# A quarter's shift and scale as one 512-wide row product, and four other edits, in a one-core transformer block

## The chip, the cores and the metric

The kernel runs on one core of one Trainium2 chip. The metric is device time in microseconds (us) of the whole program: the median of 3 runs before is 2113.18 us (2111.8 to 2114.73). Five engines work side by side: TensorE (PE, with its weight loads shown as PEld), VectorE (DVE), ScalarE (ACT), GpSimd (POOL) and SyncE (SP, which here only issues DMAs). Each has its own list of instructions and waits on semaphores for the others. Matrix products are written to PSUM, in tiles of up to 128 partitions x 512 floats; everything else on the core lives in SBUF.

## The reference, cut to what matters

```python
cond = jax.nn.silu(c)
mod = (cond @ ada_w[l] + ada_b[l]).reshape(B, N_SUBLAYERS, 3, D_MODEL)
h = modulate(x, norm_g[l, 0], mod[:, 0, 0], mod[:, 0, 1])      # rms_norm(x) * g * (1 + scale) + shift
x = x + 0.5 * mod[:, 0, 2][:, None, :] * swiglu(h, ffn1_w1[l], ffn1_w3[l], ffn1_w2[l])
h = modulate(x, norm_g[l, 1], mod[:, 1, 0], mod[:, 1, 1])
y = hybrid_mixer(h, ...)     # FoX attention and DSA attention, two gates, output product
x = x + mod[:, 1, 2][:, None, :] * y
h = modulate(x, norm_g[l, 2], mod[:, 2, 0], mod[:, 2, 1])
x = x + 0.5 * mod[:, 2, 2][:, None, :] * swiglu(h, ffn2_w1[l], ffn2_w3[l], ffn2_w2[l])
```

The model width D is 1024, there are 1024 positions, and the feed-forward width is 2816. `mod` needs nine 1024-wide products of one row (`cond`) with `ada_w`, 4 MB for each of the nine. All of it is float32.

## The kernel before, in words

**Layout.** x is held transposed: eight tiles of 128 channels, each in two halves of 512 positions (`x[c][half]`). A precise product is made of three reduced-precision ones (`mm3`): each operand is split into a high part `wh` or `h` (ACT rounds it) and a low part `wl` or a second `h` (DVE subtracts). These products read a float32r type; a few small ones are taken in plain float32: the row products of the modulation, the column sums of the norm and the spreading of the norm factor. The two feed-forward layers use Strassen-like block products with seven operands (`Operands`, `UpPair`, `Down`).

**Who sets the order.** The kernel records all operations of a stage in a `Plan` and then places them engine by engine with its own cost table (`Plan.length`, durations in us) before it emits them. Each engine then runs that fixed list. All instructions show one line, L198, in the profile, so they are told apart by tile names. Within the first stage the DMA issues of SP are kept in the written order up to `nc.inorder = False`.

**The start.** SP first loads `c` (tile `cond`), then the eight first halves of x (256 KB each). ACT's queue loads `ada_b` and `ng`. ACT makes Silu of `cond` and squares the x tiles (`nacc`, `nsq`), DVE adds the squares, and PE sums them over partitions by four products with `ones_col`; DVE makes the inverse root (`nv`, `na`, `nr`, twelve small operations one after another), and PE spreads it over all partitions by four products with `ident`. The result is `rb`.

Before the first layer can start, shift and scale of the first 256 channels are needed (quarter 0: x tiles 0 and 1), and soon after, those of quarter 1 (tiles 2 and 3). For each quarter eight 256 KB loads bring 1024 rows x 256 columns of `ada_w` twice, for shift (i = 0) and scale (i = 1). In the kernel before, `ModQuarter.row` makes the shift on PE: eight float32 products of one weight column (`cond`) with 256 columns of `mraw`, accumulated in one row; ACT copies the row (`mrow`) and two products with `ones_col` turn it into columns. `ModQuarter.add` makes the scale on DVE: eight multiply-adds over 128 x 256 (`macc`), summed over partitions by two products. `mod_done` adds the bias and, for the scale, forms A = (1 + scale) * g.

Then `Operands.block(c)` makes the operand pair: DVE computes x = x * A * rb in one pass, ACT the high part h = x + shift, DVE the low part. From then on PE runs `y<-h,wh` and `y<-h,wl` products of the first layer.

**The end of attention.** `attention` walks blocks j of 256 positions for pairs of heads; `att_values` turns the weights (`pt`, then `pth` on ACT and `ptl` on DVE), multiplies them with the values (`vst`) into a PSUM tile `py` of two buffers, which the gates share, and takes it out by ACT and DVE (`yt`). The first operation of the next stage is the last gate, 24 products into a bank of tag `b`.

**The end.** `Down.run` finishes the last feed-forward layer. In its last pass (p = 6) the last 3 of 11 weight pairs are done block by block: 9 products of 512 columns, one `xc` operation on DVE, and a 256 KB store to the output.

Of the kernel before, what the change touches and what calls it, by code (L numbers as in the profile page):

```python
# [23 lines left out]
D = 1024  # L24
# [153 lines left out]
class Plan:  # L178
# [111 lines left out]
    def length(self, t, e):  # L290
# [1167 lines left out]
def attention(k, p, kind, npairs, out, ps2, ps_t, ps_y):  # L1458
# [79 lines left out]
class ModQuarter:  # L1538


    N = 256

    def __init__(self, k, i, q, bank):
        self.k, self.i, self.q, self.bank, self.raws = k, i, q, bank, []

    def load(self, g):
        k, n = self.k, self.N
        t = t512(k, name="mraw")
        c0 = self.i * D + self.q * n
        k.nc.sync.dma_start(t.rearrange("p (a n) -> p a n", a=2),  # L1550
                            k.ada_w[g * 256:g * 256 + 256, c0:c0 + n].rearrange("(a p) n -> p a n", p=128))
        self.raws += [t[:, 0:n], t[:, n:2 * n]]

    def add(self):
        k, nc = self.k, self.k.nc
        acc = t512(k, name="macc")[:, 0:self.N]
        for kc, t in enumerate(self.raws):
            c = k.cond[:, kc:kc + 1]
            if kc == 0:
                nc.vector.tensor_scalar(acc, t, c, None, op0=ALU.mult)  # L1560
            else:
                nc.vector.scalar_tensor_tensor(acc, t, c, acc, op0=ALU.mult, op1=ALU.add)
        self.done(acc, k.ones_col)

    def row(self):
        k, nc = self.k, self.k.nc
        t = self.bank()[0:1, 0:self.N]
        for kc, r in enumerate(self.raws):
            nc.tensor.matmul(t, k.cond[:, kc:kc + 1], r, start=kc == 0, stop=kc == 7)
        r = t512(k, name="mrow")[0:1, 0:self.N]  # L1570
        nc.scalar.activation(r, t, AF.Copy)
        self.done(r, k.ones_col[0:1, :])

    def done(self, v, one):
        t = self.bank()
        for b in range(2):
            self.k.nc.tensor.matmul(t[:, b:b + 1], v[:, b * 128:b * 128 + 128], one, start=True, stop=True)
        mod_done(self.k, self.i, t, 2 * self.q, 2)
# [32 lines left out]
class Operands:  # L1611
# [26 lines left out]
    def block(self, c):  # L1638

        self.scale(c, 0)  # L1640
        self.pair("b11" if c < 4 else "b21", self.x[c][0], self.shift(c), "h0")

# [237 lines left out]
class Down:  # L1880
# [87 lines left out]
    def run(self, steps={}):  # L1968

        k = self.k  # L1970
        for p, (first, _, early) in enumerate(self.ORDER):
# [11 lines left out]
            def mms(d, q):  # L1983
                w, m = ops[q]
                c = slice(d * 128, d * 128 + 128)
                mm3(k, ps[d], w[0][:, c], w[1][:, c], *m, new and q == 0, q == PAIRS - 1, skip_group_check=True)
# [17 lines left out]
            for d in range(4):  # L2004
                for q in range(together, PAIRS):
# [217 lines left out]
def layer(tc, xT, c, pos, ada_w, ada_b, ng, inv, w13a, w2a, w_a, w_f, w_q, w_g, fb, fg, dg, wbr, wout, w13b, w2b, out):  # L2223
    with ExitStack() as es:
# [64 lines left out]
        with ExitStack() as ph:  # L2289
# [24 lines left out]
            quarter = [[ModQuarter(k, i, q, bank) for i in range(2)] for q in range(2)]  # L2314
# [49 lines left out]
            for i in range(8):  # L2364
# [4 lines left out]
                                    channel_multiplier=1)  # L2369
            sq = SquareSum(k, nc.vector)  # L2370
# [5 lines left out]
            for n in range(4):  # L2376
                for m in quarter[0]:
                    m.load(n)
            for i in range(2):
                pairs[i].load1("c", (0,))  # L2380
            for n in range(4):
                for m in quarter[1]:
                    m.load(n)
# [3 lines left out]
            rms[0] = norm_rms(k, sq.acc, rp, bank)  # L2387
            ops.rb[0] = norm_spread(k, rms[0], bank)
# [160 lines left out]
        with ExitStack() as ph:  # L2549
# [10 lines left out]
            def dsa():  # L2560
# [4 lines left out]
                yield from attention(k, ap, "dsa", 4, k.d_y[1], p2, pt, py)  # L2565
# [11 lines left out]
        with ExitStack() as ph:  # L2577
# [19 lines left out]
            last_gate(k, w_g[15], bank)  # L2597
# [37 lines left out]
            for _ in rest:  # L2635
# [6 lines left out]
                        lambda t, i, j: lambda: nc.sync.dma_start(out[i, :, j * H:j * H + H], t), nc.vector)  # L2642
# [75 lines left out]
```

## Time and profile before

| What | Value |
|---|---|
| median of 3 runs | 2113.18 us (2111.8 to 2114.73) |
| profiled execution, its own time | 2112.17 us |
| its span, first to last instruction | 2110.5 us |
| PE busy | 2094.6 us, 10296 records |
| DVE, ACT, POOL busy | 1641.7, 1135.6, 251.1 us |
| first `y<-h,wh` product of the first layer | 20.89 us |
| last product ends, DVE's last operation starts | 2106.57 us |

The profiled execution is 1.67 us longer than its span (what lies around the program) and 1.01 us shorter than the median of the runs. A record is one row of the trace. One float32r product leaves one record. PE's busy time counts the modelled ends of pipelined products; the distance between starts tells the true pace.

### The profile page before, as it was taken

How to read it: one execution, taken by the hardware profiler on the slowest of the kernel's cores; microseconds unless marked ns; L12 is line 12 of the kernel's file. 1: busy time of each engine (PE TensorE's matmuls, PEld its weight loads, DVE VectorE, ACT ScalarE, POOL GpSimd, SP SyncE). 2: the span in 40 equal slices, each digit the busy share in tenths (PEclk: the TensorE clock that was granted, in tenths of full speed). 3: DMA queues.
4: the chain of work that ended last, by engine and by line, in shares of the span. 5: the costliest groups of instructions: out<-in, count | busy, mean ns of one | idle time of the engine just before them, and what ended most of it. 6: DMA issues, size and time to landing. Idle time of an engine off the chain costs nothing.

```text
span 2110.5 us, 30999 instructions
## 1 busy us (share of the span) xinstructions
PE 2094.6 (99%) x10296; PEld 1728.2 (82%) x10296; DVE 1641.7 (78%) x3167; ACT 1135.6 (54%) x2075; POOL 251.1 (12%) x397
## 2 busy tenths in 40 slices
PE   8999999999999999999999999999999999999999
PEld 5887888888888888888888888888888888888887
DVE  7989887869977399886998877979975765568554
ACT  5754444445456266688776776335543333334443
POOL 0022222321100000000444332000000000000000
PEclk9999999999999999999999999999999999999999
DMA  9468888899721555668543224794142523375511
GB/s 347 134 215 275 303 295 274 277 379 366 261 92 48 172 174 192 217 244 274 192 158 99 86 66 160 252 315 154 46 130 100 194 85 129 101 264 206 189 50 41
DMA packets 218285, 398.72 MB, mean 189 GB/s; under 512 B 27198, under 2 KB 69694, under 8 KB 217100
## 3 DMA queue, kind: packets, MB, share of 16 engines
q1 hardware_dynamic: 199772, 339.24, 48.0%
q0 software_dynamic: 18064, 57.46, 7.1%
q8 instruction: 81, 1.33, 0.3%
q14 instruction: 80, 0.66, 0.1%
q10 hardware_dynamic: 288, 0.05, 0.0%
HBM read 282.62 MB, written 114.03 MB: 188 GB/s over the span
## 4 chain that ended last, share of the span: by engine, by line
PE 91%; issue 3%; DVE 2%; DMA 2%; ACT 1%; POOL 1%; SPq 0%; POOLq 0%; DVEq 0%; ACTq 0%
PE b L198 37%; PE y L198 28%; PE pj L198 12%; PE py L198 7%; PE p L198 4%; PE pt L198 4%; DMA mraw<-in_ada_w 0%; POOL d_g L198 0%; DMA f<-d_f 0%; DMA wr<-in_w13b 0%; ACT nt L198 0%; DMA d_wf10l<-pre 0%; DVE z L198 0%; DMA x<-in_xT 0%; ACT h L198 0%
## 5 line engine op out<-in xcount | busy, mean ns | idle before, releaser
L198 PE MATMUL b<-h,wh 128*128 128x512 f32 x1408 | 436.5, 390 | 0.5 <-DVE z L198 0.4
L198 PE MATMUL y<-h,wh 128*128 128x512 f32 x1280 | 397.1, 390 | 0.4 <-ACT h L198 0.3
L198 ACT ACTIVATE wh<-wr 128x512 fp32r<-128x512 f32 x308 | 192.6, 629 | 316.0 <-PE b L198 166.1
L198 PEld LDWEIGHTS b<-h,wh 128*128 128x128 f32 x1408 | 263.2, 188 | 59.1 <-DVE z L198 3.4
L198 PEld LDWEIGHTS y<-h,wh 128*128 128x128 f32 x1280 | 239.6, 188 | 53.4 <-issue 1.2
L198 DVE TENSOR_TENSOR wl<-wr,wh 128x512 fp32r<-128x512 f32 x308 | 208.4, 686 | 94.4 <-ACT wh L198 88.8
L198 PE MATMUL b<-h,wl 128*128 128x512 f32 x704 | 273.6, 389 | 0.0
L198 PE MATMUL y<-h,wl 128*128 128x512 f32 x640 | 249.0, 389 | 0.0
L198 PE MATMUL pj<-wh,h 128*128 128x512 f32 x512 | 161.3, 391 | 0.0
L198 PEld LDWEIGHTS b<-h,wl 128*128 128x128 f32 x704 | 132.2, 188 | 27.7
L198 PEld LDWEIGHTS y<-h,wl 128*128 128x128 f32 x640 | 120.1, 188 | 24.8
L198 ACT ACTIVATE wh<-g 128x512 fp32r<-128x512 f32 x154 | 96.0, 624 | 80.2 <-PE b L198 55.7
L198 PE MATMUL b<-wh 128*128 128x512 f32 x352 | 137.0, 389 | 0.7 <-ACT mrow L198 0.7
L198 DVE TENSOR_TENSOR wl<-a,wh 128x512 fp32r<-128x512 f32 x132 | 90.8, 688 | 59.9 <-ACT wh L198 55.7
L198 PE MATMUL b<-wl,wh 128*128 128x512 f32 x352 | 136.9, 389 | 0.0
L198 PE MATMUL b<-wh,wl 128*128 128x512 f32 x352 | 136.8, 389 | 0.0
L198 ACT ACTIVATE wh<-a 128x512 fp32r<-128x512 f32 x132 | 82.4, 625 | 99.9 <-PE b L198 60.3
L198 DVE TENSOR_TENSOR wl<-g,wh 128x512 fp32r<-128x512 f32 x154 | 105.6, 686 | 29.6 <-ACT wh L198 29.1
L198 POOL TENSOR_SCALAR pr<-pr,mn 128x128 f32<-128x128 f32 (+7 forms) x128 | 102.3, 816 | 167.3 <-DVE mn L198 135.1
L198 ACT ACTIVATE pth<-pt 128x512 fp32r<-128x512 f32 (+1 forms) x160 | 85.5, 554 | 55.9 <-PE pt L198 54.3
L198 DVE TENSOR_TENSOR ptl<-pt,pth 128x512 fp32r<-128x512 f32 (+1 forms) x160 | 97.9, 632 | 20.1 <-ACT pth L198 18.6
L198 PEld LDWEIGHTS pj<-wh,h 128*128 128x128 f32 x512 | 95.7, 188 | 18.6
(382 smaller groups left out, 4376.4 us busy)
## 6 DMA issues: line engine op xcount, KB each, us to landing
g<-d_g SPq DMA_DIRECT2D x154, 256.0 KB, 5.3
mraw<-in_ada_w SPq DMA_DIRECT2D x144, 256.0 KB, 5.7
wr<-in_w13a SPq DMA_DIRECT2D x112, 256.0 KB, 5.4
wr<-in_w13b SPq DMA_DIRECT2D x88, 256.0 KB, 4.8
d_g<-z POOLq DMA_DIRECT2D x77, 256.0 KB, 5.8
d_g<-z SPq DMA_DIRECT2D x77, 256.0 KB, 3.2
a<-in_w2a SPq DMA_DIRECT2D x44, 256.0 KB, 6.3
a<-in_w2b SPq DMA_DIRECT2D x44, 256.0 KB, 5.3
```

The costliest lines, as they stand in the source:

```text
L198: getattr(getattr(self.tc.nc, engine), op)(*map(real, a), **{n: real(v) for n, v in kw.items()})
```

## The change

Six edits, and one entry of the planner's cost table.

- `ModQuarter` is replaced by `Quarters`: a load now brings 128 rows with 256 columns of shift and 256 of scale side by side, and PE makes both in one row of 512 by eight float32 products. Nothing of it is left on DVE. ACT copies the 512-wide row, four products turn it into columns, and `mod_done` is called for scale and shift.
- x * rb (`normed`) is done before A is known. After A, ACT makes h = x * A + shift directly from it, and DVE makes x * A apart and then the low part (`rounded`). This holds for x tiles 0 to 3.
- `cond` is loaded by ACT's queue, `ada_b` and `ng` by POOL's; SP begins with x.
- The value products of the last block of DSA attention go to a half of a `p2` tile and not to `py`; the last gate uses a bank of tag `y`.
- The last block of the last pass is done in two halves of 256 columns, each with its own DVE operation and 128 KB store.
- The planner's cost of a plain float32 product becomes max(0.112, 0.005 + n / 1200) us for n columns; it was max(0.224, 0.009 + n / 595), with 1200 in place of 595 for a one-row result.

```diff
-                d = max(0.224, 0.009 + n / (595.0 if t.rows > 1 else 1200.0))
+                d = max(0.112, 0.005 + n / 1200.0)
...
-    yield from att_values(k, p, *pend, ps_t, ps_y)
+    yield from att_values(k, p, *pend, ps_t, ps_last or ps_y)
...
-class ModQuarter:
...
+class Quarters:
+    def load(self, kc):
+        k, c = self.k, self.q * 256
+        t = t512(k, name="mraw")
+        src = k.ada_w[kc * 128:kc * 128 + 128, 0:2 * D].rearrange("p (i n) -> p i n", i=2)
+        k.nc.sync.dma_start(t.rearrange("p (i n) -> p i n", i=2), src[:, :, c:c + 256])
+        self.raws.append(t)
+
+    def sums(self):
+        t = self.bank()
+        for kc, w in enumerate(self.raws):
+            nc.tensor.matmul(t[0:1, :], k.cond[:, kc:kc + 1], w, start=kc == 0, stop=kc == 7)
+        self.row = t512(k, name="mrow")[0:1, :]
+        nc.scalar.activation(self.row, t[0:1, :], AF.Copy)
+
+    def columns(self):
+        for b in range(4):
+            nc.tensor.matmul(t[:, b:b + 1], r[:, b * 128:b * 128 + 128], k.ones_col[0:1, :], start=True, stop=True)
+        for i in (1, 0):
+            mod_done(k, i, t[:, 2 * i:2 * i + 2], 2 * self.q, 2)
...
+    def normed(self, c):
+        t = self.x[c][0]
+        self.k.nc.vector.tensor_mul(t, t, self.rb[0])
+
+    def rounded(self, c):
+        nc.scalar.activation(a, t, AF.Identity, bias=shift, scale=scale)
+        self.x[c][0] = x = t512(k, name="x")
+        nc.vector.tensor_scalar(x, t, scale, None, op0=ALU.mult)
+        nc.vector.scalar_tensor_tensor(b, x, shift, a.bitcast(F32), op0=ALU.add, op1=ALU.subtract)
...
+                if p == 6 and self.s == 2 and d == 3:
+                    for i in range(2):
+                        cs = slice(i * 256, i * 256 + 256)
+                        for q in range(together, PAIRS):
+                            mms(d, q, (cs,))
+                        k.nc.vector.scalar_tensor_tensor(t[:, cs], ps[d][:, cs], g, t[:, cs], op0=ALU.mult, op1=ALU.add)
+                        self.done(t[:, cs], d, 1, i)()
+                    break
...
-        k.cond = const_in([128, 8], "cond", c)
-        k.ada_b = const_in([128, 72], "ada_b", ada_b, nc.scalar)
-        k.ng = const_in([128, 24], "ng", ng, nc.scalar)
+        k.cond = const_in([128, 8], "cond", c, nc.scalar)
...
+            k.ada_b = const_in([128, 72], "ada_b", ada_b, nc.gpsimd)
+            k.ng = const_in([128, 24], "ng", ng, nc.gpsimd)
...
-            for m in quarter:
-                m[1].add()
-                m[0].row()
+            for c in range(2):
+                ops.normed(c)
+            quarter[0].columns()
+            for c in range(2, 4):
+                ops.normed(c)
+            quarter[1].sums()
+            quarter[1].columns()
             for c in range(4):
-                ops.block(c)
+                ops.rounded(c)
...
-                yield from attention(k, ap, "dsa", 4, k.d_y[1], p2, pt, py)
+                yield from attention(k, ap, "dsa", 4, k.d_y[1], p2, pt, py, lambda: p2()[:, 0:H])
...
-            last_gate(k, w_g[15], bank)
+            last_gate(k, w_g[15], k.seed_bank)
```

Since the planner sets the order, the lists of the engines move too. The middle of the program (mixer projections, indexer, top-k and nearly all of attention) keeps its order. Two places matter below.

PE at the start, from the first row product on (`mraw` is the loaded piece of `ada_w`, `nacc` the sum of squares, `nr` the norm factor, `mrow` and `macc` the results that are turned into columns). Before:

```order
L198 MATMUL b<-mraw,cond 1x256 x2
L198 MATMUL b<-ones_col,nacc 128x1 x4
L198 MATMUL b<-mraw,cond 1x256 x6
L198 MATMUL b<-ones_col,mrow 128x1 x2
L198 MATMUL b<-ident,nr 128x128 x4
L198 MATMUL b<-ones_col,macc 128x1 x2
L198 MATMUL b<-mraw,cond 1x256 x2
L198 MATMUL y<-h,wh 128x512 x2
L198 MATMUL b<-mraw,cond 1x256 x2
L198 MATMUL y<-h,wh 128x512 x3
```

Now:

```order
L198 MATMUL b<-ones_col,nacc 128x1
L198 MATMUL b<-mraw,cond 1x512
L198 MATMUL b<-ones_col,nacc 128x1 x3
L198 MATMUL b<-mraw,cond 1x512 x5
L198 MATMUL b<-ident,nr 128x128 x2
L198 MATMUL b<-mraw,cond 1x512
L198 MATMUL b<-ident,nr 128x128 x2
L198 MATMUL b<-mraw,cond 1x512
L198 MATMUL b<-ones_col,mrow 128x1 x4
L198 MATMUL y<-h,wh 128x512
L198 MATMUL b<-mraw,cond 1x512
L198 MATMUL y<-h,wh 128x512
```

All eight products of quarter 0 now stand ahead of the first `y<-h,wh`, at twice the width, and the first of them behind a product that waits for the sum of squares. Before, quarter 0 had its eight at 256 columns there and quarter 1 its first two. The eight of quarter 1 now stand singly between the first `y` products.

PE at the end of attention (`pr` are the weights to be turned, `gw` is the last gate's weight). Before:

```order
L198 MATMUL pt<-ident,pr 128x128 x2
L198 MATMUL py<-ptl,vst 64x256
L198 MATMUL py<-ptl,vst 64x128
L198 MATMUL pt<-ident,pr 128x128 x3
L198 MATMUL py<-pth,vst 128x256 x2
L198 MATMUL py<-pth,vst 128x128
L198 MATMUL py<-ptl,vst 64x256
L198 MATMUL py<-ptl,vst 64x128
L198 MATMUL py<-pth,vst 128x128
L198 MATMUL py<-ptl,vst 64x256
L198 MATMUL py<-ptl,vst 64x128
L198 MATMUL b<-h,gw 128x512 x24
```

Now:

```order
L198 MATMUL pt<-ident,pr 128x128 x3
L198 MATMUL py<-ptl,vst 64x256
L198 MATMUL py<-ptl,vst 64x128
L198 MATMUL py<-pth,vst 128x128
L198 MATMUL p_14551<-pth,vst 128x256 x2
L198 MATMUL p_14551<-pth,vst 128x128
L198 MATMUL p_14551<-ptl,vst 64x256
L198 MATMUL p_14551<-ptl,vst 64x128
L198 MATMUL p_14551<-ptl,vst 64x256
L198 MATMUL p_14551<-ptl,vst 64x128
L198 MATMUL p_14551<-pth,vst 128x128
L198 MATMUL y<-h,gw 128x512 x24
```

The last eight value products go to another tile and end with a `pth` product, where before they ended with two `ptl` products. On ACT the two takings-out (`yt`) now stand behind all `pth` copies; before, one stood between them.

More of the change, by code (lines that the diff above doesn't have):

```diff
@@ L1455, in pair_heads, with attention @@
     k.ready = heads
-def attention(k, p, kind, npairs, out, ps2, ps_t, ps_y):
+def attention(k, p, kind, npairs, out, ps2, ps_t, ps_y, ps_last=None):
     pend = ()
@@ L1535, in steps @@
         mod_done(k, self.i, cols, 4 * self.h, 4)
-class ModQuarter:
[L1541 to L1547, printed above, removed]
-        t = t512(k, name="mraw")
[L1549 to L1554, printed above, removed]
-        k, nc = self.k, self.k.nc
[L1556 to L1574, printed above, removed]
-        t = self.bank()
-        for b in range(2):
-            self.k.nc.tensor.matmul(t[:, b:b + 1], v[:, b * 128:b * 128 + 128], one, start=True, stop=True)
-        mod_done(self.k, self.i, t, 2 * self.q, 2)
@@ new lines, with __init__ @@
+class Quarters:
+    def __init__(self, k, q, bank):
+        self.k, self.q, self.bank, self.raws = k, q, bank, []
+    def load(self, kc):
+        k, c = self.k, self.q * 256
+        t = t512(k, name="mraw")
+        src = k.ada_w[kc * 128:kc * 128 + 128, 0:2 * D].rearrange("p (i n) -> p i n", i=2)
+        k.nc.sync.dma_start(t.rearrange("p (i n) -> p i n", i=2), src[:, :, c:c + 256])
+        self.raws.append(t)
+    def sums(self):
+        k, nc = self.k, self.k.nc
+        t = self.bank()
+        for kc, w in enumerate(self.raws):
[3 more added lines that the diff above has]
+    def columns(self):
+        k, nc, r = self.k, self.k.nc, self.row
+        t = self.bank()
[3 more added lines that the diff above has]
+            mod_done(k, i, t[:, 2 * i:2 * i + 2], 2 * self.q, 2)
@@ L1641, in block @@
         self.pair("b11" if c < 4 else "b21", self.x[c][0], self.shift(c), "h0")
+    def normed(self, c):
+        t = self.x[c][0]
+        self.k.nc.vector.tensor_mul(t, t, self.rb[0])
+    def rounded(self, c):
+        k, nc, t, i = self.k, self.k.nc, self.x[c][0], self.s * 8 + c
+        scale, shift = k.A[:, i:i + 1], self.shift(c)
+        a, b = t512(k, F32R, "h", "h0"), t512(k, F32R, "h", "h0")
+        nc.scalar.activation(a, t, AF.Identity, bias=shift, scale=scale)
+        self.x[c][0] = x = t512(k, name="x")
+        nc.vector.tensor_scalar(x, t, scale, None, op0=ALU.mult)
+        nc.vector.scalar_tensor_tensor(b, x, shift, a.bitcast(F32), op0=ALU.add, op1=ALU.subtract)
+        k.B["b11"].append((a, b))
     def first(self):
@@ L1981, in run, with mms @@
             ops = []
-            def mms(d, q):
+            def mms(d, q, cut=(slice(0, H),)):
                 w, m = ops[q]
                 c = slice(d * 128, d * 128 + 128)
-                mm3(k, ps[d], w[0][:, c], w[1][:, c], *m, new and q == 0, q == PAIRS - 1, skip_group_check=True)
+                for s in cut:
+                    mm3(k, ps[d][:, s], w[0][:, c], w[1][:, c], m[0][:, s], m[1][:, s], new and q == 0, q == PAIRS - 1, skip_group_check=True)
             together = PAIRS - self.APART.get(p, 0)
@@ L2313, in layer @@
             mod = {i: ModHalf(k, i, 1, bank) for i in range(2)}
-            quarter = [[ModQuarter(k, i, q, bank) for i in range(2)] for q in range(2)]
+            quarter = [Quarters(k, q, bank) for q in range(2)]
             k.up_step, k.stores = 0, []
@@ L2375, in layer @@
                     nc.tensor.matmul(warm, z.bitcast(F32)[:, 0:128], x[i][0], start=True, stop=True)
-            for n in range(4):
-                for m in quarter[0]:
-                    m.load(n)
+            for n in range(8):
+                quarter[0].load(n)
             for i in range(2):
                 pairs[i].load1("c", (0,))
-            for n in range(4):
-                for m in quarter[1]:
-                    m.load(n)
+            for n in range(8):
+                quarter[1].load(n)
             for i in range(2, 4):
@@ L2387, in layer @@
             rms[0] = norm_rms(k, sq.acc, rp, bank)
+            quarter[0].sums()
             ops.rb[0] = norm_spread(k, rms[0], bank)
-            for m in quarter:
-                m[1].add()
-                m[0].row()
+            for c in range(2):
[5 more added lines that the diff above has]
+            quarter[1].columns()
             for c in range(4):
-                ops.block(c)
+                ops.rounded(c)
             for i in range(4):
```

3 lines of the change are left out of this document (2 added, 1 removed).

## The prediction

> **What bounds the kernel now.** I read the page first, then the busy time by stretch, then the chain of waits at the start, at the end of attention and at the end.
>
> ```profile
> span 2110.5 us, 30999 instructions
> PE 2094.6 (99%) x10296; PEld 1728.2 (82%) x10296; DVE 1641.7 (78%) x3167; ACT 1135.6 (54%) x2075; POOL 251.1 (12%) x397
> ```
>
> PE works 99% of the span. An average hides where the rest is, so the stretches follow (start:end, length, then busy us of PE, PEld, DVE, ACT, POOL).
>
> ```profile
> 0.00:21.00 21.00, 15.43 (x57) 7.55 (x57) 13.63 (x39) 10.25 (x17) 1.16 (x7) 1.00 0.92 303
> 21.00:36.50 15.50, 15.50 (x68) 10.30 (x69) 13.18 (x27) 5.38 (x10) 0.00 (x0) 1.00 1.07 379
> 36.50:460.00 423.50, 422.53 (x1871) 346.50 (x1869) 359.09 (x609) 218.62 (x382) 104.02 (x191) 1.00 0.78 270
> 460.00:735.00 275.00, 274.00 (x1245) 230.40 (x1245) 199.61 (x364) 143.52 (x253) 27.11 (x54) 1.00 0.56 198
> 735.00:1000.00 265.00, 264.34 (x1219) 219.10 (x1220) 228.01 (x632) 192.40 (x344) 0.00 (x0) 1.00 0.64 218
> 1000.00:1300.00 300.00, 297.62 (x2276) 250.10 (x2275) 254.23 (x580) 225.07 (x492) 117.58 (x143) 1.00 0.36 113
> 1300.00:1303.00 3.00, 1.74 (x13) 1.31 (x12) 1.73 (x4) 1.09 (x2) 0.61 (x1) 1.00 0.95 311
> 1303.00:2106.60 803.60, 803.48 (x3556) 662.91 (x3554) 571.49 (x917) 339.23 (x578) 0.61 (x1) 1.00 0.46 155
> ```
>
> From 21 us on PE has almost no idle time: 0.97, 1.00, 0.66, 2.38, 1.26 and 0.12 us in the last six stretches, 6.4 us in all. So each microsecond added to PE's work after 21 us, and each by which its steady run starts later, should reach the end. Only the start, the end of attention and the very end are set by other engines. The start:
>
> ```profile
> 15.39 1.04 PE b L198 x4
> ...
> 16.45 0.38 ACT mrow L198
> ...
> 16.88 2.04 PE b L198 x16
> ...
> 18.95 0.17 DVE mod L198
> ...
> 19.14 0.17 DVE A L198
> ...
> 19.34 0.76 DVE x L198
> ...
> 20.12 0.73 ACT h L198
> ...
> 20.89 0.73 PE y L198 x2
> ```
>
> PE waits for the last piece of the shift until 15.39; 5.5 us later the first layer starts. DVE's multiply-adds for the scale run beside this: the second `mod`, which is theirs, follows PE's work without a gap.
>
> **The price of a plain float32 product** decides the case. Rows of one stretch, grouped by form, and of PE's timeline (start, length, count):
>
> ```profile
> L198 PE MATMUL b<-mraw,cond 128*1 128x256 f32 x32 | 8.0, 378 | 2.3 <-DMA mraw<-in_ada_w 2.3
> ...
> 7.91 1.88 PE L198 MATMUL b<-x,zr 128*128 128x512 f32 x4
> ...
> 12.05 1.05 PE L198 MATMUL b<-ones_col,nacc 128*128 128x1 f32 x8
> 13.03 1.89 PE L198 MATMUL b<-mraw,cond 128*1 128x256 f32 x8
> ...
> 17.41 1.16 PE L198 MATMUL b<-ident,nr 128*128 128x128 f32 x8
> ```
>
> The list of PE holds 16 products of `mraw`, the trace 32 records; four products with `nacc` leave 8 records, four with `ident` 8. So a plain float32 product is two records. At 13.03 eight records of 256 columns take 1.89 us, the last of them 0.38: (1.89 - 0.38) / 7 = 0.216 us from start to start, 0.43 us a product. The one form of 512 columns, `b<-x,zr`, stands 0.43 us from start to start ((1.88 - 0.59) / 3, the last one 0.59), 0.86 us a product. The rows of 256 and of 512 give one pace, so I take 0.86 us for a 1x512 product. Eight cost 6.9 us of PE, where the eight of 256 cost 3.45. The planner now believes 0.43.
>
> **The change part by part.**
>
> *Constants to other queues.* SP's first DMA was `cond`:
>
> ```profile
> 0.81 0.39 SPq L198 DMA_DIRECT2D cond<-in_c  x1
> 1.25 3.75 SPq L198 DMA_DIRECT2D x<-in_xT  x8
> ```
>
> x and all behind it start 0.44 us earlier (1.25 - 0.81); I take it for the landings too, as the queue behind is paced by landings, with bounds 0 and 0.44. `ada_b` and `ng` wait behind two short POOL operations and are needed after 20 us: nothing.
>
> *Quarter 0.* PE's first product of the sum of squares moves from 12.05 to 11.6, and the first row product now stands behind it. From there PE has, in a row, eight 1x512 products (6.9), four with `nacc` and four with `ident` (0.22 each by the rows above, 1.8) and some six changes of kind (0.05 each, 0.3): it ends at 20.6. Nothing delays it further: the last piece of the shift is there at 15.39 now, and PE reaches the seventh of the eight at 18.4; the norm factor is ready near 16, twelve DVE steps of 0.2 us (as `mod` and A stand apart) after 13.6, while PE reaches `ident` at 17.8. What follows:
>
> ```profile
> L198 ACT ACTIVATE mrow<-b 1x512 f32<-1x512 f32 x12 | 7.0, 584 | 12.5 <-PE b L198 12.2
> ...
> L198 ACT ACTIVATE nt<-nt,mod,A 128x512 f32<-128x512 f32 x16 | 12.8, 808 | 6.1 <-DVE nt L198 6.1
> ```
>
> The result is out 0.16 us after the last record's pace, the copy takes 0.58 (21.4), four products into columns 1.05 (22.45), three small DVE steps 0.2 each (23.1), and ACT's h with both a scale and a bias column 0.81, as `nt` does now. The first `y<-h,wh` starts at 24.0 and not at 20.89: +3.1 us. The early x * rb saves DVE's 0.76 between A and h; that is in this sum, and so is the DVE work that is gone. The added x * A on DVE, four at no more than the 0.76 of the pass they are split from, lies beside PE's row products: the low part that needs it is asked for only after two more of them.
>
> *Quarter 1.* Behind the first `y` product PE had three groups of two row products left, 2.6 us; now it has eight of 512, 6.9 us: +4.3. Each insertion among `y` products costs something too:
>
> ```profile
> 21.56 1.02 PE L198 MATMUL b<-mraw,cond 128*1 128x256 f32 x4
> 22.51 0.96 PE L198 MATMUL y<-h,wh 128*128 128x512 f32 x3
> ```
>
> Four records worth 0.86 took 0.95 until the next `y`, and about as much is lost on the way in: 0.2 a time, and there are four more of them (nine for five): +0.8. The columns cost the same (four products then, four now). PE is at 15.50 of 15.50 us busy in this stretch, so all of it counts.
>
> *Start in all: +8.2 us* (6.5 if changes of kind are free and the landings gain more; 9.5 if ACT and DVE answer late).
>
> *End of attention.* The chain there:
>
> ```profile
> 1298.88 0.60 ACT yt L198
> ...
> 1299.53 0.39 PE py L198 x2
> 1299.92 0.34 PE pt L198 x3
> ...
> 1300.29 0.50 ACT pth L198
> ...
> 1300.83 0.90 PE py L198 x6
> ...
> 1301.76 0.60 ACT yt L198
> ...
> 1302.40 0.39 PE py L198 x2
> ```
>
> Twice PE's `ptl` products wait for ACT's `yt` of the same tile, and once for a `pth` that stood behind `yt`. In the new order all `pth` copies come first and no `ptl` product stands behind a `yt`. What is left is ACT, DVE, PE once each: I get 1301.1 for the last product where it was 1302.6, 1.5 us less. The next stage splits on ACT and DVE what DMA brings at its own pace, so some may be lost there again: I count -1.3, between -0.3 (most is) and -2.2 (all 1.26 us idle of 1300 to 1303 and the 0.6 of the first `yt` go).
>
> *The end.*
>
> ```profile
> 2106.15 0.39 PE L198 MATMUL y<-wh,wl 128*128 128x512 f32 x1
> 2106.57 0.75 DVE L198 SCALAR_TENSOR_TENSOR xc<-y,G,xc 128x512 f32<-128x512 f32 x1 [1.29 <-PE y L198]
> 2107.35 0.33 SPq L198 DMA_DIRECT2D out_dram<-xc  x1
> ...
> L198 DVE SCALAR_TENSOR_TENSOR macc<-mraw,cond,macc 128x256 f32<-128x256 f32 x14 | 6.7, 482 | 0.2
> ```
>
> DVE's last operation falls from 0.75 to some 0.48 (-0.27); the store of half the size lands up to 0.35 earlier (I take 0.15); 18 products of 256 columns for 9 of 512 cost nothing if only columns count and +0.9 if each of the nine more costs 0.1, as a change of kind does; between equal kinds I take +0.1. Together -0.3 (-0.6 to +0.5). The earlier half is hidden behind the second half's products.
>
> *Order elsewhere.* Both feed-forward layers are placed anew. Their PE idles 0.97 us in 423 and 0.12 in 804, so there is little to win: 0, between -1 and +2.
>
> **Sum:** 8.2 - 1.3 - 0.3 = +6.6 us. The profiled execution took 2112.17 us, so 2118.8 on its terms; the median of the runs lies 1.0 above it, so **2119.8 us**, 0.31% slower.
>
> **The rivals.**
>
> *A 1x512 product costs half of that, so the kernel is not slower.* This is what the planner's new entry says; it decides wherever the row product stands before the first `y`. Then PE finishes quarter 0 near 17.4, the first `y` starts near 20.9 as before, quarter 1 costs +0.9 and the insertions +0.8, and with the two gains the sum is 0.1 us: 2113.3. Against it: the count of records. Chance 8%. The Trainium skill, "TensorE: Matmul & The Clock Gate", section "Back-to-back issue gap", gives some 216 ns for 512 columns; by that alone eight products would be 1.7 us, and the sum would lie below this rival's. But its page "FP8 and Floating Point Precision", section "TensorE Precision Notes", says that true FP32 takes four passes through the array, an estimate of 0.86 us a product by both; the trace agrees for 256 columns with 0.43, and no run here shows 1x512 yet.
>
> *The delay is swallowed later.* If PE comes late, its partners are ready when it comes, and its waits between 36 and 1300 us (0.97 + 1.00 + 0.66 + 2.38 = 5.0) could shrink. That needs those waits to be on work that doesn't wait for PE itself; most in attention are on ACT or DVE results of PE's own products. If all went, 2114.8; if half, 2117.3. Chance 10%.
>
> *A new wait in the reordered layers.* The planner now takes plain float32 products for half their length and plans the first and last stage on that; a `y` or `b` bank that comes free late would stop PE where it had 0.12 us of idle. At the rate of attention's stretch (2.38 in 300) 804 us lose 6.4: with half to all of that 2123 to 2126. Chance 7%.
>
> **How the numbers follow.** Forecast 75%, rivals 8, 10 and 7%. With its own bounds the forecast reaches from about 2115.5 (start 6.5, attention -2.2, the end -0.6, order -1) to 2123.5 (9.5, -0.3, +0.5, +1, less a little, as not all go wrong at once); the half-price case and the worst of the new waits are left out. A measurement tells 0.2% apart, 4.2 us: slower is above 2117.4, faster below 2109.0. Of the forecast some 0.65 of the whole lies above 2117.4; with the new wait and a little of the swallowed delay, slower is 0.74. The rest of the forecast, most of both other rivals: 0.22 the same. Faster: 0.04.
>
> **What would show it.** Sixteen products of `mraw` as 32 records of 512 columns 0.43 us apart; the first `y<-h,wh` near 24.0; PE's last `mraw` record near 33.5 (26.8 before); in PE's stretch from 1296 to 1303 under 2 us idle and the first `gw` product about 1.5 us nearer to what precedes it; the last DVE operation near 0.48 us. The forecast is wrong if a 1x512 product takes under 0.6 us, if PE idles less before 24 us by more than 2 us than I have it, or if PE's idle time after 40 us differs from 6 us by more than 3.

## The result and the profile after

| | before | after |
|---|---|---|
| median of 4 runs each, us | 2112.6 (2111.8 to 2114.73) | 2125.68 (2124.26 to 2127.55) |
| ratio, 95% interval | | 1.0061 (1.0043 to 1.0078) |
| profiled execution, its span, us | 2112.17, 2110.5 | 2125.6, 2123.9 |

The change makes the kernel 0.6% slower: 13.1 us between the medians and 13.4 between the spans, where 6.6 were forecast. The page of the kernel after begins:

```profile
span 2123.9 us, 31056 instructions
PE 2106.4 (99%) x10305; PEld 1729.7 (81%) x10305; DVE 1634.6 (77%) x3156; ACT 1135.3 (53%) x2075; POOL 251.6 (12%) x399
```

PE's busy time grew by 11.8 us and the span by 13.4. To see where, I took the start of the same PE record in both traces; the difference is the lag. "Product 24" counts the first layer's `y<-h` and `b<-h` products from 0.

| PE record | before, us | lag after, us |
|---|---|---|
| first `y<-h,wh` | 20.89 | +5.72 |
| product 24 | 31.20 | +12.94 |
| product 100 | 50.26 | +12.93 |
| first attention scores | 1001.27 | +12.95 |
| first branch product `b<-yh,wh` | 1308.15 | +11.22 |
| last branch product `y<-yh,wh` | 1394.54 | +12.23 |
| late in the last layer, `b<-wh` | 2043.81 | +12.82 |
| last product | 2106.15 | +13.88 |
| span | 2110.45 | +13.41 |

Nearly everything is lost before 45 us. Over the 970 us that follow, the lag ends as it began. The end of attention wins 1.73 of it; the branches (1.01), the stretch up to the end of the last layer (0.59) and the last block (1.06) add to it, and the tail gives 0.47 back. PE's timeline of the start after (start, length, operation, count; in brackets the idle time and what ended it):

```profile
8.52 1.02 PE L198 MATMUL b<-x,zr 128*128 128x512 f32 x2
12.24 0.38 PE L198 MATMUL b<-ones_col,nacc 128*128 128x1 f32 x2 [2.71 <-DVE nacc L198]
12.55 1.02 PE L198 MATMUL b<-mraw,cond 128*1 128x512 f32 x2
...
14.26 6.15 PE L198 MATMUL b<-mraw,cond 128*1 128x512 f32 x10
...
24.27 1.05 PE L198 MATMUL b<-ones_col,mrow 1*128 1x1 f32 x8 [0.68 <-ACT mrow L198]
26.61 0.50 PE L198 MATMUL y<-h,wh 128*128 128x512 f32 x1 [1.30 <-ACT h L198]
...
28.42 1.87 PE L198 MATMUL b<-mraw,cond 128*1 128x512 f32 x2
```

Two records of a row product take 1.02 us at 12.55 (0.43 to the second, and 0.59 for it) and 1.87 at 28.42. Ten take 6.15 at 14.26, where nine paces of 0.43 and a last one of 0.59 make 4.46. So some rows run at half pace, and the view by stretches says why. I cut it at the points where the granted clock changes; the columns are as in the prediction, and the one after the five engines is the granted clock.

```profile
7.89:11.31 3.42, 1.65 (x4) 0.38 (x2) 2.69 (x4) 2.88 (x5) 0.00 (x0) 1.00 1.07 370
11.31:14.72 3.41, 2.48 (x12) 1.24 (x13) 1.09 (x4) 0.00 (x0) 0.00 (x0) 1.00 1.11 351
14.72:18.13 3.41, 3.41 (x6) 0.51 (x5) 1.65 (x11) 0.00 (x0) 0.00 (x0) 0.50 1.06 377
18.13:21.54 3.41, 3.41 (x12) 0.92 (x10) 0.00 (x0) 0.00 (x0) 0.00 (x0) 1.00 1.10 348
...
24.96:28.37 3.41, 2.11 (x8) 0.73 (x7) 2.98 (x8) 3.34 (x6) 0.00 (x0) 1.00 1.06 389
28.37:31.79 3.42, 3.42 (x6) 0.67 (x6) 3.19 (x6) 0.00 (x0) 0.00 (x0) 0.50 1.05 387
```

Twice PE got half its clock for 3.41 us while it had work, each time behind a stretch in which it had stood idle for a while. Before, the clock was 1.00 in every stretch of the profiled execution. The loss is about 1.7 us a time. The kernel before is not free of such stretches either: of its 33 executions timed beside four of the later experiments, 18 show a mean granted clock of 1.0 (median 2112.63 us), 11 of 0.999 (2113.87) and 4 of 0.998 (2114.95); the four of the changed kernel show 0.997 to 0.999. The chain of waits before the first `y` after:

```profile
12.24 11.37 PE b L198 x32
...
23.63 0.59 ACT mrow L198
24.21 1.56 ACT wh L198 x3
25.77 0.79 ACT h L198
...
26.61 0.50 PE y L198
```

ACT's h stands behind three weight roundings `wh` that the list has put there. They cost nothing: A, which h needs too, leaves DVE at 25.71.

### The profile page after: what moved, and what is told of

The parts are those of the page before. It is cut to its first block, busy times and chain, and to the rows that moved or that the text cites. A ratio compares the mean times of both kernels' runs of the same rounds, so it can differ in the third digit from the quotient of the medians.

```text
span 2123.9 us, 31056 instructions
## 1 busy us (share of the span) xinstructions
PE 2106.4 (99%) x10305; PEld 1729.7 (81%) x10305; DVE 1634.6 (77%) x3156; ACT 1135.3 (53%) x2075; POOL 251.6 (12%) x399
## 4 chain that ended last, share of the span: by engine, by line
PE 94%; DVE 2%; ACT 1%; DMA 1%; issue 1%; SPq 0%; DVEq 0%; ACTq 0%
PE b L198 38%; PE y L198 30%; PE pj L198 12%; PE py L198 7%; PE p L198 4%; PE pt L198 4%; DVE h L198 0%; ACT nt L198 0%; DMA h<-d_y 0%; ACT h L198 0%; DVE nacc L198 0%; DMA x<-in_xT 0%; SPq L198 0%; DMA mraw<-in_ada_w 0%; DMA f<-d_f 0%
```

## The experiments

Each kernel was timed against the kernel before on the same chip. The medians of before lie between 2113.07 and 2114.02 us there, so ratios are compared, and not microseconds of different groups. Lags are against the trace of before used above.

### The start put back, and the start alone

The changed kernel with the old start:

```diff
-            quarter = [Quarters(k, q, bank) for q in range(2)]
+            quarter = [[ModQuarter(k, i, q, bank) for i in range(2)] for q in range(2)]
```

(with its loads, `add`, `row` and `ops.block` in place of `normed` and `rounded`).

> The changed kernel with the start of before put back (the two separate rows of 256, two of the four halves summed on DVE, A and the norm factor in one DVE pass); the moved constants, the last value products, the planner's cost entry and the halved last block stay as changed. Theory S (the start alone carries the loss, as the traces line up: +12.9 us at product 24 of the first layer, then -1.6 at the attention end, +1.0 in the branches, +0.8 and +0.8 later, -0.5 in the tail): first y<-h,wh again near 20.9 (up to 21.5, since the constants still share the transfers with x), PEclk 1.00 from 14.5 to 18.1 and from 28.4 to 32.0, time 2112.6 + 0.5 = about 2113 (2111.5 to 2114.5). Rival O (the new cost entry reorders the layers and that costs some us): 2117 to 2121, with the lag growing between products 24 and 800 of the first layer.

Measured: 2120.86 us (2120.55 to 2122.19), ratio 1.0033 (1.0020 to 1.0046). Theory S falls: the start is the old one and still 7.9 us late at product 24. Rival O has the time right and the place wrong: from product 24 to attention the lag goes from 7.9 to 7.3, so nothing is lost in the layers. PE's first `mraw` row is not at 10.95 as before but behind the norm factor, at 19.24.

The other way round, the kernel before with only the new start (the diff of the change without its other parts):

> The kernel before with only the new start (one row of 512 for shift and scale, normed and rounded); constants on their old queues, old cost entry, old attention end, old last block. Theory S: +12 to +13 us, 2124.6 to 2126, the granted clock halved once or twice before 32 us, rows 0.43 us apart where it is not. Rival C (the constants on GpSimd's queue hold up x, which empties PE's queue and brings the halved clock): with the constants where they were, the clock stays at 1.00 and the loss is the +8.2 us of the prediction, 2120.8 (2119.5 to 2122).

Measured: 2119.69 us (2118.69 to 2123.93), ratio 1.0033 (1.0020 to 1.0046). +9.49 at product 24, with one halved window from 14.51 to 17.92. Three of the five executions show a mean granted clock of 1.0 and took 2118.69 to 2119.69; the two at 0.999 and 0.998 took 2123.37 and 2123.93. That is more than the 1.7 us of the one halved window; the profiled execution, one of these two, lost another 1.66 between product 24 and attention. The number is rival C's, but the next two runs show that it isn't the constants. Theory S, which had 2124.6 to 2126, falls here too. So each of two parts loses most of the time alone: 7.9 and 9.5 with, together, 12.9.

### The cost entry alone, and the rest without start and entry

What the run with the old start still had of the change and could move PE's list was the planner's entry. The kernel before with one line:

```diff
-                d = max(0.224, 0.009 + n / (595.0 if t.rows > 1 else 1200.0))
+                d = max(0.112, 0.005 + n / 1200.0)
```

> The kernel before with one line changed: the planner's cost entry for an unrounded product. Theory P (the entry, which halves the planner's price of the 128x1 products and leaves the rows' alone, pulls the row products of the start behind the norm factor's, PE then stands idle and the granted clock is halved, as in the run with the old start): first y<-h,wh at 26 to 27.5, PE idle from 9 to 12 and from 13 to 17 us, two or three halved windows, +7 to +8 at product 24, time 2119 to 2122. Rival Q (the constants on GpSimd's queue made that run slow, the entry did nothing): first y<-h,wh near 20.9, 2112 to 2114.5.

Measured: 2121.98 us (2120.49 to 2123.47), ratio 1.0043 (1.0028 to 1.0058). One line of the planner costs 8.4 us. PE's timeline of this run:

```profile
12.19 1.05 PE L198 MATMUL b<-ones_col,nacc 128*128 128x1 f32 x8 [2.28 <-DVE nacc L198]
17.16 2.04 PE L198 MATMUL b<-ident,nr 128*128 128x128 f32 x8 [3.92 <-DVE nr L198]
...
19.35 4.15 PE L198 MATMUL b<-mraw,cond 128*1 128x256 f32 x14
...
27.32 0.96 PE L198 MATMUL y<-h,wh 128*128 128x512 f32 x3 [1.92 <-ACT h L198]
```

The list now has PE wait for the norm factor (3.92 us) before it touches rows whose data lie there; in the kernel before twelve records of `mraw` filled that time. The clock is halved from 14.52 to 21.34 and from 28.17 to 31.59. PE has work from 17.16 on, so I estimate from these figures that (4.18 + 3.42) / 2 = 3.8 us of the +8.56 at product 24 are the clock's and the rest the new order's. The end of this execution is +10.93, as another 2.3 us went behind the branches, with one more halved window from 1465.18 to 1468.60. Theory P holds, though the loss at product 24 is 0.56 over its range. Rival Q falls: here the constants are on their old queues.

The changed kernel with the old start and the old entry, that is, the constants' queues, the end of attention and the halved last block alone:

> The changed kernel with the old start and the old cost entry, so that of the change only the constants' queues, the last value products with the last gate's banks, and the halved last block stay. Theory P: start within 0.6 of before, attention end -1.2 to -1.6, branches +0.8 to +1.3 given back, last block +1.0, tail -0.5; together 0 to +1.2: 2112.5 to 2114.5. Rival Q (late x and late constants): PE idle before the first row product, lag +2 to +5 at product 24, 2116 to 2119.

Measured: 2112.31 us (2110.78 to 2114.05), ratio 0.9995 (0.9986 to 1.0004). First `y` at 20.92, +0.03 at product 24: the constants do no harm and bring nothing. Theory P holds for the start; the time is 0.2 under its range. From attention's first scores the lag runs +0.55, -1.28 (first branch product), -0.53 (last one), -0.82 (late in the last layer), +0.23 (last product), -0.23 (span).

### The new start with the old entry

> The changed kernel with the old cost entry alone put back. Theory P: PE's order of the start is that of the run with only the new start, so +7.8 us at product 24 where no window is halved and 1.7 more for each that is: +7.8 to +11.2; with +0.5 for what follows 2121 to 2124. Rival N (the entry matters in the old start alone): +12.9 and 2125.7 as the changed kernel.

Measured: 2120.07 us (2118.2 to 2122.34), ratio 1.0035 (1.0021 to 1.0049). Its profiled execution has a granted clock of 1.00 throughout:

```profile
11.91 1.05 PE L198 MATMUL b<-ones_col,nacc 128*128 128x1 f32 x8 [2.60 <-DVE nacc L198]
12.90 5.31 PE L198 MATMUL b<-mraw,cond 128*1 128x512 f32 x12
...
22.82 1.88 PE L198 MATMUL b<-mraw,cond 128*1 128x512 f32 x4
24.73 0.73 PE L198 MATMUL y<-h,wh 128*128 128x512 f32 x2
```

(5.31 - 0.59) / 11 = 0.43 us a record: the price of the prediction. The first `y` is 3.84 late, product 24 is 7.23 late, a little under the 7.8 expected and the 8.2 of the prediction's sum. Here two products of quarter 1 run at 22.82, while DVE and ACT make h; in the changed kernel PE idles there (`1.30 <-ACT h`). So the entry costs in the new start too. Rival N falls; theory P has the place right, but the time lies 0.9 us under its 2121 to 2124. A wait of this length does not always halve the clock: PE waited 2.60 us here, in the changed kernel 2.71.

### PE kept busy

The changed kernel with four more products that nothing reads:

```diff
-                if i < 4:
+                if i < 8:
                     nc.tensor.matmul(warm, z.bitcast(F32)[:, 0:128], x[i][0], start=True, stop=True)
```

> The changed kernel with four more of the products that already run on arriving x tiles (128x512, weights zero, nothing reads them), so that PE is busy on x4 to x7 in the hole from 9.5 to 12.2 us. Theory K (the granted clock falls to half for 3.41 us because PE stood idle before): no halving at 14.7 to 18.1, the four row records there 0.43 and not 0.85 apart, first y<-h,wh 1.5 to 1.9 earlier (24.7 to 25.1), time -1.7 (2123.9), or -3.4 (2122.3) if the second halving goes too. Rival W (these records are slow because they wait for their data or a bank): still 0.85 apart, first y not earlier, time 2125.7 to 2126.5.

Measured: first `y` at 24.60 (2.01 earlier), +9.39 at product 24 instead of +12.94, both halved windows gone. Theory K holds in the place it speaks of, and in this trace the two windows were worth 3.55 us. But the time is 2125.3 us (2124.37 to 2126.04), ratio 1.0052 (1.0035 to 1.0069), an interval that overlaps the changed kernel's, and the span is only 0.57 shorter, where theory K had 3.4. In its trace the gain is kept to the first branch product (+8.12 where the change has +11.22) and then lost, in part to another halved window, at the norm of the last layer, where PE waits 1.07 us for a sum of squares:

```profile
1463.77:1467.18 3.41, 2.34 (x15) 2.03 (x15) 3.13 (x10) 0.92 (x2) 0.00 (x0) 1.00 0.41 153
1467.18:1470.60 3.42, 3.42 (x10) 2.64 (x9) 2.21 (x9) 1.07 (x2) 0.00 (x0) 0.50 0.02 5
```

With two more such products, on the normed x2 and x3:

```diff
+            for c in (2, 3):
+                nc.tensor.matmul(bank(), z.bitcast(F32)[:, 0:128], x[c][0], start=True, stop=True)
             quarter[1].sums()
```

> As the last, and two more such products on the normed x2 and x3, which fall in the holes from 23.4 to 24.3 and from 25.3 to 26.6 us. Theory K: PEclk 1.00 in all windows to 40 us, both slow stretches gone; -3.4 us, less up to 0.9 where an added product stands ahead of the columns: 2122.3 to 2123.2. Rival W: no gain, and the added 1.7 us of products show: 2125.7 to 2127.4.

Measured: 2124.51 us (2123.97 to 2125.32), ratio 1.0048 (1.0034 to 1.0063). The clock is 1.00 in every stretch, here the two that were at half:

```profile
14.70:18.10 3.40, 3.40 (x13) 1.22 (x14) 1.96 (x12) 0.00 (x0) 0.00 (x0) 1.00 1.06 375
...
28.40:32.00 3.60, 3.60 (x10) 0.83 (x10) 2.29 (x4) 0.00 (x0) 0.00 (x0) 1.00 1.05 386
```

+10.23 at product 24: 3.55 less for the clock, some 0.8 more for a product that stands ahead of the columns. The span keeps 1.6 of these 2.7 us; 1.05 went in the first layer after product 24. The times alone, whose intervals overlap, don't show the gain. The mean clocks of all executions do show that the windows went: 1.0 in three of four here, 0.997 to 0.999 in the four of the changed kernel. In the run before this one they are 0.998 and 0.999, so there the trace stands alone. Rival W falls in both runs, since the rows are 0.43 apart.

The same tried from the other side, on the kernel before, where PE's list stays as it was but for two products left out:

```diff
-                if i < 4:
+                if i < 2:
                     nc.tensor.matmul(warm, z.bitcast(F32)[:, 0:128], x[i][0], start=True, stop=True)
```

> The kernel before without two of its four products on arriving x tiles (x2 and x3; nothing reads them), the order of all else as before: PE is idle from about 6.4 to 10.95 us instead of from 9.5. Theory K (an idle stretch of PE halves the granted clock for 3.41 us or twice that): one or two halved windows between 10 and 18 us, the rows there 0.43 instead of 0.22 apart, first y<-h,wh later by 1 to 4 us and the time by as much: 2114.5 to 2117.5. Rival W (idle time of PE here costs nothing but itself): clock 1.00, first y<-h,wh at 20.9, time as before, 2112 to 2114.5.

Measured: 2115.56 us (2114.09 to 2117.58), ratio 1.0010 (1.0001 to 1.0019), +2.80 at the first `y` and at product 24. Less work makes it slower:

```profile
8.52:11.93 3.41, 0.65 (x4) 0.28 (x4) 2.98 (x5) 2.42 (x4) 0.00 (x0) 1.00 1.06 374
11.93:15.34 3.41, 3.41 (x13) 2.12 (x12) 2.05 (x9) 0.00 (x0) 0.00 (x0) 0.50 1.11 351
15.34:18.76 3.42, 3.42 (x9) 1.01 (x8) 3.28 (x14) 0.00 (x0) 0.00 (x0) 0.50 1.06 375
```

Theory K holds in the trace, with the size expected. The times don't show it: the five executions at a mean clock of 0.998 have a median of 2115.70 us and the four at 1.0 one of 2114.89 (2114.16 to 2117.33), where the kernel before has 2112.63 at 1.0. So most of the 2 us between the medians has another cause than the clock. The lag of the profiled execution grows by another 1.9 us between product 24 and attention, on waits for DVE that I did not follow up.

### Half the row products

What was left of the start, +7.2, is by the prediction the row products' own time. The run with the old entry, with every second row product left out, so that shift and scale are sums over half of the input:

```diff
-            nc.tensor.matmul(t[0:1, :], k.cond[:, kc:kc + 1], w, start=kc == 0, stop=kc == 7)
+            if kc % 2:
+                nc.tensor.matmul(t[0:1, :], k.cond[:, kc:kc + 1], w, start=kc == 1, stop=kc == 7)
```

> The changed kernel with the old cost entry (the run that lay +7.2 us at product 24 with the clock at 1.00) and only every second of the eight row products of each quarter (slabs 1, 3, 5 and 7; the other four are loaded and left out, so the shift and scale are sums over half of the input). Theory R (what is left of the start's loss is the row products' own time on PE, 0.86 us each): 8 x 0.86 = 6.9 us less, 3.4 of it before the first y<-h,wh (near 21.3) and 3.4 behind it: +0.3 at product 24, time 2113 (2112 to 2115). Rival L (the loss is latency: copy, columns, A and h one after the other, or the arrival of the last slab at 15.4): at most the 3.4 behind the first y go, first y<-h,wh stays near 24, time 2116 to 2118.

Measured: first `y` at 21.60, 3.13 earlier than with all products; +3.39 at product 24, 3.84 less. The time is 2117.97 us (2115.9 to 2119.23), ratio 1.0020 (1.0011 to 1.0030). Ahead of the first `y` theory R is right to 0.3 us. Behind it only 0.7 more was won, for two reasons. Two of the products left out had lain in the hole at 22.82 and had cost nothing there. And PE now had too little to do before h came, and the next window was halved:

```profile
18.15:21.56 3.41, 1.05 (x8) 0.96 (x8) 2.55 (x9) 3.28 (x7) 0.00 (x0) 1.00 1.10 349
21.56:24.98 3.42, 3.38 (x5) 1.14 (x6) 3.42 (x7) 0.69 (x1) 0.00 (x0) 0.50 1.08 366
```

With half of these 3.42 us added back, 3.84 + 1.7 = 5.5 us were won by six products that counted, 6 x 0.86 = 5.2. Rival L falls by the start, though the time lies in its range and 3 us over theory R's: at the beginning of attention this execution lost another 3.3 us (+2.84 to +6.1), with a wait of 2.01 for `nat` from memory and a window at half clock from 1011.43 to 1014.84. Why it waited there I did not find.

### The end of attention

The changed kernel with the last value products in `py` and the last gate's bank as before:

```diff
-            last_gate(k, w_g[15], k.seed_bank)
+            last_gate(k, w_g[15], bank)
```

> The changed kernel with the last value products in their old place and the last gate's banks as before. Theory G (the 1.6 us won at the attention end are given back where the branches wait for yl from DVE): lag at the first yh product as large as at the start of attention, no new stall in the branches, so at the last yh product 0.3 to 1.0 more than the changed kernel: time +0.3 to +1.0, 2126 to 2127. Rival B (the stalls in the branches come from the banks that the last gate now takes, or from the cost entry's order): they stay, 1.6 more at the last yh product: 2127.3. Rival U (the whole edit is worth its 1.6): same time as rival B, but with the stalls gone in neither.

Measured: 2125.16 us (2124.32 to 2127.52), ratio 1.0060 (1.0045 to 1.0075); the times can't tell it from the changed kernel. The traces can. PE's busy time in two stretches of ten microseconds, first of this run, then of the changed kernel:

```profile
1310.00:1320.00 10.00, 7.78 (x50) 6.41 (x49) 4.88 (x9) 4.95 (x10) 2.40 (x5) 1.00 0.74 203
1320.00:1330.00 10.00, 10.00 (x45) 8.19 (x44) 8.67 (x14) 8.63 (x15) 0.00 (x0) 1.00 1.05 397
```

```profile
1310.00:1320.00 10.00, 9.86 (x57) 8.13 (x56) 4.90 (x9) 4.69 (x10) 1.45 (x3) 1.00 0.88 260
1320.00:1330.00 10.00, 9.56 (x41) 7.25 (x41) 9.18 (x14) 9.11 (x15) 0.00 (x0) 1.00 1.05 396
```

With the old end PE waits at the end of attention and never in the branches. With the new one it waits in the branches. From attention's first scores to the last branch product the lag moves by -0.28 (14.41 to 14.13; the start of this execution has three halved windows) in this run and by -0.72 in the changed kernel: the edit is worth some 0.4 us in its place. Theory G holds. U falls, and of B the part on the entry's order, which this run has as well. The last gate's bank went back together with the value products, so the run can't acquit it; but PE's only waits in the branches are for `yl` (0.4 us), not for a bank. What stops PE in the branches, by the chain of the changed kernel:

```profile
1313.44 6.46 DMA h<-d_y
...
1319.93 0.63 ACT yh L198
1320.58 0.60 ACT gt L198
1321.18 0.53 ACT yh L198
...
1321.79 0.70 DVE yl L198
...
1322.54 1.66 PE b L198 x6
```

The values come back from memory at DMA's pace, and ACT takes the last gate out (`gt`) between two of them. PE came earlier, the data did not. The next run shows it against the kernel before: its first branch product starts 1.36 us earlier, while ACT's first three `yh` start at 1304.27, 1306.46 and 1307.34, before at 1303.94, 1306.16 and 1307.01.

The same edit alone on the kernel before, and with a fifth product on an arriving x tile (`if i < 5`):

> The kernel before with only the last value products and the last gate moved to the other banks. Theory G (won at the attention end, mostly given back in the branches): lag -1.5 to -2.0 at the first yh product, -0.4 to -1.1 at the last one and at the end: time -0.4 to -1.1, 2112 to 2113. Rival U (the whole is kept): -1.6 to -1.9.

> The last kernel with one more product on an arriving x tile (x4), which fills PE from 9.6 to 10.5 us and leaves 0.5 of the idle 1.2 us. Theory K: fewer executions with a halved window (mean granted clock 1.0 in all runs where before shows 0.998 to 1.0), the median nearer the fast end: -1 to -2 against before, 2111 to 2112.5. Rival: the one product moves nothing, same as the run without it.

Measured: 2112.35 us (2111.58 to 2114.18), ratio 0.9994 (0.9985 to 1.0003), and 2111.84 us (2110.32 to 2113.12), ratio 0.9992 (0.9983 to 1.0001). Neither is shown to be faster than before; these are the lowest ratios of the study. The first one's lags go +0.45, -1.36, -0.31, +0.18: won 1.8, given back 1.05, as theory G has it. The end at +0.18 is outside its range, as 0.49 were lost behind the branches. Of the second, nine of eleven executions have a mean clock of 1.0, but so have nine of eleven of the first, and its profiled one has a halved window (20.42 to 23.83). So the fifth product did nothing that I can show, and that 2111.84 lies in theory K's range is luck.

### The true price in the planner's entry

> The kernel before with the planner's entry set to what the trace shows for every unrounded product, rows too: two records, n/595 us, at least 0.224. Theory P (the entry sets the start's order, and an order is good only if PE has row products to run before the norm factor): two row products stay ahead of the norm products, no long hole at 12 us, but the row's columns go behind the norm factor's, first y<-h,wh 0 to 1.5 later: 2112.5 to 2115.5. Rival (a true price makes a better order): 2109 to 2111.5.

Measured: 2116.61 us (2114.98 to 2117.01), ratio 1.0014 (1.0006 to 1.0023), above the 2115.5 that theory P gave at most, and the rival falls. At product 24 it is +0.04, as P said. The loss is later in the first layer: -0.10 at product 1200, +1.54 at product 1500, +4.62 at attention's first scores, on waits for ACT's `wh` (1.9 us) that the other orders don't have. A truer price made a worse order, and my theory, which looked at the start alone, did not see it.

## Why the prediction was right or wrong

The sign was right and the size was half: +6.6 forecast, +13.4 between the spans. By the prediction's own terms:

| Term | forecast | measured |
|---|---|---|
| start | +8.2 | +12.94 |
| end of attention with the branches | -1.3 | -0.72 |
| order elsewhere | 0 | +0.59 |
| last block and store | -0.3 | +0.59 |
| between product 24 and attention | 0 | +0.01 |

**The price of the 1x512 product held:** two records, 0.43 us apart wherever the clock is 1.00, and the first `y` comes 3.13 us earlier when four of them are left out ahead of it (4 x 0.86 = 3.4). The rival of half that price falls.

**The step that failed is the start's sum, "Start in all: +8.2 us (6.5 ... 9.5)".** It added up durations at full clock. With the clock at 1.00 in the whole start the same order takes +9.39 (the run with four more products), inside the range. The other 3.55 are the two windows at half clock, for which the sum had no term, though its list of PE showed the row products moved behind the norm's, and with that a PE that has nothing to do from 9.5 to 12.2. Without them the spans would be 9.9 us apart, which is 2123.0 beside the median of 2113.18, just within the forecast's bounds; this is an estimate from the lags. The Trainium skill, "TensorE: Matmul & The Clock Gate", section "What's actually happening", says that the array's clock is halved behind an idle window of some 3.4 us, on a grid that does not start with the kernel. The traces agree on the length (3.41 to 3.42 us) and that the grid lies elsewhere in each execution. They don't agree on "idle": windows with PE busy for 2.48, 2.11 and 2.34 us were followed by a halved one. The prediction left the rule out; by its words nothing would have happened here, since PE's longest idle time in the start is 2.71 us.

**The 1.2 us between 8.2 and 9.4** are the first `y` (24.60 where I had 24.0; the landings that I counted 0.44 earlier gave 0.02 at the first `nacc` product, 12.03 against 12.05, and 11.65 to 12.24 in the other traces with the moved constants, but for one with another order) and quarter 1 (15.99 us from the first `y` to product 24, 5.68 more than before, where 4.3 + 0.8 were counted).

**The planner's entry** had no term in the prediction. It left the price of a 1x512 row as it was (0.436 to 0.432 us) and halved that of the products with 128 rows, so "takes plain float32 products for half their length" is right for these alone. It was the costliest single line: +8.4 us alone in the old start, and 2.2 us of the new one (9.39 less 7.23, both at full clock; the first has the added products, so this is a rough size). The prediction took the changed order as given and did not ask what the new start would cost in the old one.

**End of attention:** won 1.73, forecast 1.5; "some may be lost there again" was 1.01, and I had counted 0.2. Within the bounds given.

**The bounds** do not add up as stated: the lower parts give 2115.9 and not 2115.5, and with the +2 of "order elsewhere" in place of 1 the upper ones give 2124.9, less a little. 2125.68 lies above that as well.

**The end:** DVE's last operation fell to 0.48 and the tail by 0.47, near the 0.42 forecast. What failed is "the earlier half is hidden behind the second half's products". The timeline after:

```profile
2118.47 0.28 PE L198 MATMUL y<-wh,wl 128*128 128x256 f32 x1
2118.79 0.48 DVE L198 SCALAR_TENSOR_TENSOR xc<-y,G,xc 128x256 f32<-128x256 f32 x1 [0.68 <-PE y L198]
2119.33 0.39 PE L198 MATMUL y<-wh 128*128 128x256 f32 x1 [0.58 <-DVE xc L198]
...
2120.34 0.48 DVE L198 SCALAR_TENSOR_TENSOR xc<-y,G,xc 128x256 f32<-128x256 f32 x1 [1.07 <-PE y L198]
```

Both halves lie in one PSUM tile. Of the 18 products, twelve stand ahead of the wait, so three of the second half's; DVE starts on the first half only behind the twelfth, and the last six start only when DVE has read it: 0.86 us from 2118.47 to 2119.33 where 0.12 is the pace. From the record at 2043.81 to the last product, all eight kernels with the halved block lose 1.05 to 1.06, and those without it nothing. PE's wait is for a semaphore that DVE's operation raises, so the program asks for it; whether the chip would need it for two halves of one tile was not tried.

**The rivals.** "Swallowed later" fell: +12.94 at 31 us and +12.95 at 1001. "A new wait in the reordered layers" named 2123 to 2126, and 2125.68 lies in it, but not for its reason: of 13.4 us, 0.59 lie between the branches and the end of the last layer, and the first layer adds nothing. Even the 0.59 are not shown to be the reorder's: with the attention edit alone, whose PE list there is as before, the same stretch took 0.49 more, and with only the new start 0.16.

**What the runs leave open** is why a window is halved: PE was busy for 1.65 us in the window from 7.89 to 11.31 of the changed kernel and the next one had the full clock; 2.48 us in the one after, and the next was halved. In the run with the old entry 2.35 us were followed by the full clock, in the kernel before 2.47 and 2.45. So busy time alone does not tell.

## What to carry to other kernels

A planner's cost table is part of the kernel: a change of one price moved work that was free out of a hole and alone cost about as much as the new start alone (ratios 1.0043 and 1.0033), so order a change to it alone and look at who stands idle. Where PE waits between bursts of small products, as here for 1.3 to 2.7 us, price the microseconds after the wait at half clock too, and see what could fill the hole. A wait removed ahead of a stage that is paced by transfers can come back inside that stage, as 1.05 of 1.8 us did here, so follow the lag to the end of the next stage before counting the gain.

## What the runs showed of the hardware that I had not expected

- The granted clock falls to 0.50 for 3.41 us, or twice that, behind windows in which PE was still busy for 0.65 to 2.48 of 3.41 us; other windows with 1.65 to 2.47 us were followed by the full clock.
- In the traces, taking away two products that nothing reads costs 2.8 us at the first layer, and adding four takes 3.55 away.
- The windows lie on a grid that is elsewhere in each execution (the first change of the clock after 8 us at 14.72, 14.51, 14.52, 13.67 and 11.93 us in five traces), so what falls into a halved window, and with it the time, differs between executions of one program: the kernel before took 2112.63 us in the median of 18 executions at a mean clock of 1.0, and 2114.95 in that of four at 0.998.
- A product of 256 columns follows the one before it after 0.12 us; with a wait for DVE between them, 0.86 us passed, though DVE itself worked for only 0.48 of them.
